# A planner inside the kernel: VectorE and GpSimd excluded from each other, new durations, and layer 0's leftover work carried into layer 1's plan

## The chip, the core and the metric

The kernel runs on one core of one Trainium2 chip. The metric is the device time of one launch in microseconds (us); the median of three runs is used. Short names: PE is TensorE (matmuls), DVE is VectorE, ACT is ScalarE, POOL is GpSimd, SP is SyncE, which only issues DMAs here.

## The reference

One inference step of a two-layer decoder trunk with model width 1024, in fp32, on 1056 tokens: a prompt of 1024, and 8 samples of 4 tokens that go on from given states. Each layer computes `x + mixer(rmsnorm(x) @ w_in) * silu(gate) @ w_out`; a last rmsnorm follows.

- Layer 0 is an RG-LRU. `w_in` maps 1024 to 2 x 1536 (the branch and its gate). The branch goes through a causal convolution of width 4 and through two gates (recurrence and input), each of 16 blocks of 96 x 96; then comes the scan `h[t] = a[t] h[t-1] + sqrt(1 - a[t]^2) * i[t] * x[t]` along the tokens, with `a = exp(-8 softplus(-lambda) r)`.
- Layer 1 is an HGRN2 with 8 heads. `w_in` maps 1024 to 4 x 1024 (q, f, i, gate). Per head a state of 128 x 128 is carried along the tokens with a decay per row, and `o = q S`. An rmsnorm per head, the silu gate and `w_out` follow.

Outputs are both `y` and the new states of both layers.

## The kernel before

**Data and products.** Everything is held transposed: 128 features on the partitions, tokens along the free axis, in three chunks of `CH` = 352 tokens. fp32 accuracy comes from three fp32r matmuls per product step (`mm3`, lines 243 to 245): each operand is split into a rounded part (`xh`, `whi`) and a rest (`xl`, `wlo`), and high x high, low x high and high x low are summed in PSUM. A product of 128 output features has 8 such steps (k = 0 to 7). Weights come by DMA (line 312), ACT casts them to `whi` (line 380), and DVE or POOL subtracts to give `wlo` (line 325, the helper `subtract`, which also makes every `xl`).

**Start of layer 0.** PE has 48 small filler matmuls (line 729), most of which run ahead of the first product. Two DMAs bring the gains and the packed parameters `P`. For chunk 0, ACT and DVE make `xh` and `xl` from the raw x (lines 861, 867), and the norm's factor is put in after the product; for chunks 1 and 2 the norm's factor is put in before. `squares` (lines 430, 432, 435) squares each x and adds up; a matmul sums over the partitions (line 279); DVE scales (line 447), POOL takes the power -1/2 (line 449), DVE builds a diagonal (lines 450, 453) and PE spreads it over the partitions (line 455). `scaled_parts` then does for each k: DVE scale (line 460), ACT cast (line 461), DVE or, for k = 3 and 7, POOL subtraction (line 325). The products are evacuated (line 482), convolved (ACT line 498, then three DVE steps on line 501) and split (lines 506, 507), or turned into gates (lines 529 to 534). `lru` (from line 539) holds the block gates, the tanh, exp and sqrt on ACT and the scan. `smalls`, `smalls1` and `masks` are 46 tiny DVE operations, with some on ACT and POOL, on `P` (tile "smalls"); they are recorded through the helper `seq` (line 734).

**Entry to layer 1.** Layer 0 ends with `out_last` and `first1` (line 708), which computes the first two projections of head 0 of layer 1; line 721 on POOL writes the gate rows `ST` (called `Gs` in layer 1). In layer 1, `own_gate` and `scale` (lines 1023 to 1045) multiply rows of a head by decays, level by level (line 1064 combines the gate rows). PE then runs four "bursts" of small matmuls per head (lines 1330 to 1345): burst 1 for levels 0 and 1, burst 2 for levels 2 and 4, burst 3 for levels 8 and 16, burst 4 for levels 32 and 64. The first three are made of `diag` (line 1052), burst 3 of `emit16` (line 1106) as well; DVE keeps their results (lines 1056, 1059) and scales the rows for the next burst. From head `HC` = 2 on, the projections use seven products in place of eight on halved token blocks (`seven`, line 1501 for the sums of their results); for these, `build` makes 56 sums of inputs on DVE (line 1368) and splits them (`parted_sum`, lines 1371 and 325).

**What sets the order.** No order is written out by hand. Every operation is recorded by `fl.add(engine, us, emit, reads, writes, prio, ...)` into a `Flow` (line 52), with an estimated duration `us` and keys that it reads and writes; dependencies come from the keys. There are two Flows, one for layer 0 with `first1`, and one for layer 1 with the tail. `Flow.run` (line 185) then orders all operations at build time:

- `plan` (line 102) is a greedy list scheduler: the engine that can start earliest takes, of its operations that are ready, the one with the smallest key. `lag` adds a hop between engines, and DMAs add a latency. `both` marks DVE operations that must not run beside POOL's: such an operation is planned longer if POOL is busy when it starts.
- `back` (line 140) plans backward and returns latest starts, which become the keys of the next plan; this is done 8 times and the best plan is kept.
- `search` (line 167) shifts the keys of a few operations planned in the first 60 us at random, 3000 times, and keeps what brings a chosen later PE operation forward. Only layer 0 uses it (`fl.run(SEARCH, 60.0)`); layer 1 calls `fl.run()`.

The order so found is what each engine's instruction stream has; nothing is reordered on the chip. Main products keep their order among each other (`main=True`); other PE work (block gates, bursts, norms) is placed between them.

Of the kernel before, what the change touches and what calls it, by code (L numbers as in the profile page):

```python
# [19 lines left out]
ALU = mybir.AluOpType  # L20
# [31 lines left out]
class Flow:  # L52
# [3 lines left out]
    HOP = 0.2  # L56
# [38 lines left out]
    def lag(self, i, j):  # L95

        a, b = self.ops[i], self.ops[j]
        if a[0] == b[0] and not a[5]:
            return 0.0
        return self.HOP + b[6] + (2.15 + a[5] / 250.0 if a[5] else 0.0)  # L100

    def plan(self, key, stop=None):
# [5 lines left out]
        free = dict.fromkeys(self.ENGINES, 0.0)  # L108
        dma = 0.0
# [4 lines left out]
        for _ in range(n):  # L114
# [6 lines left out]
            if both and free["POOL"] > t0:  # L121
                us = max(us, free["POOL"] - t0 + us - 0.13)
# [89 lines left out]
def tile_trunk(ctx: ExitStack, tc: tile.TileContext, xT, prm, hc, w0, wg, wo0, w1, wo1, s_in,  # L212
# [85 lines left out]
    with ExitStack() as l0:  # L298
# [92 lines left out]
        def product(w, xs, step=8, more=()):  # L391
# [3 lines left out]
            for s in range(0, n, step):  # L395
# [6 lines left out]
                fl.add("PE", 0.48 * len(ks), emit, (*(q for k in ks for q in (*xs[k][2], *w(k)[2])), *more), (pk,), 1, main=True)  # L402
# [34 lines left out]
        def norm(acc, own=None):  # L437
# [11 lines left out]
            fl.add("POOL", 1.2, lambda: G.tensor_tensor(r[:, :3], r[:, :3], mhalf[:, :3], op=ALU.pow), (rk,), (rk,), 0)  # L449
# [14 lines left out]
        def conv(g, head=False):  # L464

            items = []
            for j in range(3):
# [3 lines left out]
                def evac(c, ps, pk, by=None, j=j, m=m, mine=mine):  # L471
# [25 lines left out]
                    for src, dst, sh, u in parts:  # L497
                        act(u, lambda src=src, dst=dst, sh=sh: S.activation(dst, sh(src, 3), AF.Identity, bias=pc("cb", m),  # L498
                                                                         scale=pc("cw", 36 + m)), (xk, ("P",)), (tk,), 1, 0.1)
# [39 lines left out]
        def lru(g):  # L539
# [11 lines left out]
            for c in range(NCH):  # L551
# [5 lines left out]
                for i, hb in ((0, hbr), (1, hbi)):  # L557
                    for j in range(3):
# [7 lines left out]
                                                                           scale=0.5), (pk, ("sm",)), (("R", s, i, j),), 2, 0.05)  # L566
# [5 lines left out]
                                                            scale=0.5), (pk, ("sm",)), (("td", i),), 2, 0.05)  # L572
# [3 lines left out]
                for j in range(3):  # L576
                    m = 3 * g + j
                    act(CH, lambda j=j, m=m, ta=ta, ab=ab: S.activation(ab[:, j], ta[:, j], AF.Exp, bias=cn[:, m:m + 1], scale=cn[:, m:m + 1]),
                        (tak[j], ("sm",)), (("a", s, j),), 3, 0.15)
                    act(CH, lambda j=j, m=m, ta=ta: S.activation(ta[:, j], ta[:, j], AF.Tanh, bias=cp[:, m:m + 1], scale=cp[:, m:m + 1]),  # L580
                        (tak[j], ("sm",)), (tak[j],), 3, 0.15)
# [6 lines left out]
                act(3 * CH, lambda ta=ta: S.activation(ta, ta, AF.Sqrt, scale=0.25), tak, tak, 3, 2.6)  # L588
# [3 lines left out]
                for j in range(3):  # L592
# [12 lines left out]
                    fl.add("DVE", 0.9, lambda h=h, aj=aj, bj=bj, p=p: V.tensor_tensor_scan(h, aj, bj, p, op0=ALU.mult, op1=ALU.add),  # L605
# [1206 lines left out]
```

## Time and profile before

| what | value |
|---|---|
| three runs | 1072.68, 1069.47, 1072.2 us; median 1072.2 |
| profiled execution | 1069.42 us, of which the span of the instructions is 1067.3 |
| mean granted TensorE clock | 0.996 of full speed |
| instructions | 25614 |
| HBM | 71.05 MB read, 25.49 MB written |
| DMA | 103.06 MB, 97 GB/s on average |

How to read it: the span is the time from the first to the last recorded instruction, and the profiled execution's own time lies about 2 us above it. The page gives the busy time of each engine; a view by stretches gives the same for parts of the span, and a timeline gives the instructions of one engine in order, each run of like instructions with its start, its busy time, its line and shape and, in brackets, the idle time ahead of it with the instruction that ended it. A start that the text takes from a timeline is the first number of its row.

### The profile page before, as it was taken

The numbers are of one execution on the slowest core, as the hardware profiler recorded it, in microseconds if no ns is written. First come the engines' busy times: TensorE is split into PE (matmuls) and PEld (weight loads), VectorE is DVE, ScalarE is ACT, GpSimd is POOL, SyncE is SP. The second block draws the span as 40 slices with busy tenths as digits, with TensorE's granted clock in tenths as the row PEclk, the third lists the DMA queues.
The fourth block names the chain that finished last, engine by engine and source line by source line (L and its number), as shares of the span: only waits on it lengthen the run. The fifth ranks groups of instructions, "written<-read, shape, count | busy, mean of one in ns | idle before, by whom it ended". The sixth has DMA issues, their size and how long they took to land.

```text
span 1067.3 us, 25614 instructions
## 1 busy us (share of the span) xinstructions
PE 1054.5 (99%) x9964; PEld 1026.1 (96%) x9964; DVE 816.2 (76%) x1610; ACT 589.2 (55%) x1340; POOL 526.4 (49%) x601
## 2 busy tenths in 40 slices
PE   9999999999999999999989999999999999999997
PEld 9999999999999999999989999999999999999986
DVE  7999995788888689264798987877868686883436
ACT  6569656877675875243344464646464554652324
POOL 3426443444634365555657555555545455552544
PEclk9999999999999999999999999999999999999998
DMA  9201112123752585440211121212121212374204
GB/s 294 67 20 52 57 47 74 56 60 97 228 173 61 171 282 179 126 131 28 80 33 40 44 91 46 90 44 91 44 92 51 74 62 65 123 214 127 78 8 163
DMA packets 70120, 103.06 MB, mean 97 GB/s; under 512 B 9200, under 2 KB 50160, under 8 KB 70000
## 3 DMA queue, kind: packets, MB, share of 16 engines
q1 hardware_dynamic: 67696, 98.67, 29.6%
q10 hardware_dynamic: 2304, 2.77, 0.7%
q8 instruction: 78, 1.28, 0.5%
q14 instruction: 42, 0.34, 0.1%
HBM read 71.05 MB, written 25.49 MB: 90 GB/s over the span
## 4 chain that ended last, share of the span: by engine, by line
PE 90%; DVE 6%; issue 1%; DMA 1%; POOL 1%; ACT 0%; ACTq 0%; POOLq 0%; DVEq 0%
PE mm L243 25%; PE mm L244 24%; PE mm L245 24%; PE hg L1052 1%; PE hg L569 1%; PE hg L1271 1%; DVE R L1368 1%; PE hg L1217 1%; PE hg L1161 1%; PE hg L243 1%; PE hg L245 1%; PE hg L244 1%; PE hg L1273 1%; DMA wraw<-in_w_dram 1%; PE mm L1052 1%
## 5 line engine op out<-in xcount | busy, mean ns | idle before, releaser
L243 PE MATMUL mm<-xh,whi 128*128 128x352 f32 (+1 forms) x1143 | 359.5, 315 | 0.0
L244 PE MATMUL mm<-xl,whi 128*128 128x352 f32 (+1 forms) x1143 | 354.8, 310 | 0.0
L245 PE MATMUL mm<-xh,wlo 128*128 128x352 f32 (+1 forms) x1143 | 354.7, 310 | 0.0
L325 POOL TENSOR_TENSOR wlo<-wraw,whi 128x256 fp32r<-128x256 f32 (+3 forms) x184 | 199.2, 1100 | 189.7 <-ACT whi L380 104.5
L244 PEld LDWEIGHTS mm<-xl,whi 128*128 128x128 f32 x1143 | 215.8, 189 | 1.7
L243 PEld LDWEIGHTS mm<-xh,whi 128*128 128x128 f32 x1143 | 215.5, 189 | 1.8
L245 PEld LDWEIGHTS mm<-xh,wlo 128*128 128x128 f32 x1143 | 215.5, 189 | 0.0
L501 DVE SCALAR_TENSOR_TENSOR k<-xb,prm_sb,k 128x352 f32<-128x352 f32 (+2 forms) x144 | 89.2, 629 | 14.8 <-ACT k L498 10.8
L243 PE MATMUL mm<-t,whi 128*128 128x264 f32 (+1 forms) x306 | 89.4, 292 | 0.5 <-DVE k L1501 0.5
L244 PE MATMUL mm<-t,whi 128*128 128x264 f32 (+1 forms) x306 | 87.7, 287 | 0.0
L245 PE MATMUL mm<-t,wlo 128*128 128x264 f32 (+1 forms) x306 | 87.6, 286 | 0.0
L1501 DVE TENSOR_TENSOR k<-mm,k 128x264 f32<-128x264 f32 x144 | 60.4, 428 | 34.5 <-PE mm L245 32.7
L584 POOL TENSOR_TENSOR k<-X 128x352 f32<-128x352 f32 x36 | 44.4, 1243 | 45.1 <-DVE R L585 34.3
L325 POOL TENSOR_TENSOR wlo<-R,whi 128x256 fp32r<-128x256 f32 x64 | 51.8, 830 | 25.4 <-ACT whi L1428 25.4
L380 ACT CAST whi<-wraw 128x512 fp32r<-128x512 f32 (+2 forms) x83 | 45.9, 574 | 26.4 <-PE mm L244 18.7
L243 PEld LDWEIGHTS mm<-t,whi 128*128 128x128 f32 x306 | 57.6, 188 | 1.2 <-DVE k L1501 0.9
L245 PEld LDWEIGHTS mm<-t,wlo 128*128 128x128 f32 x306 | 57.6, 188 | 0.0
L244 PEld LDWEIGHTS mm<-t,whi 128*128 128x128 f32 x306 | 57.6, 188 | 0.0
L243 PE MATMUL mm<-yh,whi 128*128 128x352 f32 x153 | 49.9, 326 | 0.0
L1428 ACT CAST whi<-wraw 128x512 fp32r<-128x512 f32 x52 | 32.0, 616 | 31.7 <-PE mm L245 17.4
L244 PE MATMUL mm<-yl,whi 128*128 128x352 f32 x153 | 49.4, 323 | 0.0
L245 PE MATMUL mm<-yh,wlo 128*128 128x352 f32 x153 | 49.4, 323 | 0.0
(478 smaller groups left out, 2601.3 us busy)
## 6 DMA issues: line engine op xcount, KB each, us to landing
wraw<-in_w_dram SPq DMA_DIRECT2D x90, 256.0 KB, 2.7
wraw<-in_wo_dram SPq DMA_DIRECT2D x34, 192.0 KB, 2.5
si<-in_s_in_dram SPq DMA_DIRECT2D x8, 512.0 KB, 3.6
out_ss_out_dram<-si SPq DMA_DIRECT2D x8, 512.0 KB, 2.8
R<-in_w_dram SPq DMA_DIRECT2D x15, 256.0 KB, 2.5
sg<-x1b SPq DMA_DIRECT2D x21, 176.0 KB, 2.8
x<-sg SPq DMA_DIRECT2D x21, 176.0 KB, 1.8
R<-td SPq DMA_DIRECT2D x72, 44.0 KB, 1.9
```

The costliest lines, as they stand in the source:

```text
L243: T.matmul(out, wh, xh, start=first, stop=False)
L244: T.matmul(out, wh, xl, start=False, stop=False)
L245: T.matmul(out, wl, xh, start=False, stop=last)
L325: emit = lambda: e.tensor_tensor(b, x, a.bitcast(F32), op=ALU.subtract)
L380: act(m, lambda hi=hi, raw=raw, m=m: S.copy(hi[:, :m], raw[:, :m]), rk, (hk,), prio)
L501: dve(u, lambda src=src, dst=dst, sh=sh, k=k: V.scalar_tensor_tensor(dst, sh(src, k), pc("cw", 12 * k + m), dst, op0=ALU.mult, op1=ALU.add ...
L569: fl.add("PE", 0.62, lambda ps=ps, i=i, c=c: T.matmul(ps[:96, :CH], gs[:, i, :], ST[:96, chunk(c)], start=True, stop=True), (("gs",), *((" ...
L584: pool(CH, lambda x=x, a=a, b=b: G.tensor_tensor(x, a.bitcast(F32), b.bitcast(F32), op=ALU.add), (ak, bk), (xk,), 3)
L1052: T.matmul(ps[32 * j:32 * j + 32, n * w:n * w + w], B[:, o:o + 32], q(slice(o, o + 32)), start=True, stop=True, tile_position=(0, 32 * j))
L1161: T.transpose(ps[:, n * 128:(n + 1) * 128], row[:, a:a + 128], ident)
L1428: act(512, lambda: S.copy(hi, raw), (rk,), (hk,), 2)
L1501: dve(QT, lambda: V.tensor_tensor(o[0], z[0], u[0], op=ALU.add), (z[1], u[1]), (o[1],), 0)
```

## The change

Nothing that is computed changes; the figures by which the two Flows order the operations do.

1. **Exclusion.** A `both` operation used to be stretched by what was left of POOL's operation at its start. Now it works both ways: a `both` operation of DVE is planned longer by what is left of POOL's last operation (`taken`), and a POOL operation by what is left of the last `both` operation (`locked`). The allowance is 0.085 and 0.05 in place of 0.13.
2. **Durations.** The estimates of ACT, DVE and POOL as functions of the columns n, the hop between engines, and the costs of many single operations are set anew. `seq`, used by the small parameter operations, falls from 0.2 to 0.1 and its DVE operations lose the mark `both`. POOL's `tensor_scalar` in `first1` and in layer 1 falls to 0.3 of its length, its `memset` rises from 0.3 to 0.7.
3. **Leftover work.** Layer 1's Flow starts each engine not at zero but at the time by which its last planned operation of layer 0 ends after PE's (`busy`). An operation of POOL with no instruction and no duration writes the gate keys `GK`.
4. **Search.** Layer 1's Flow runs the random search over its first 60 us, as layer 0's did.

The list of operations that are recorded and their dependencies are otherwise the same. `SEARCH` stays at 3000.

```diff
-    HOP = 0.2
+    HOP = {"PE": 0.22, "DVE": 0.14, "ACT": 0.14, "POOL": 0.14, "SP": 0.2}
...
-    def __init__(self, until=None, side=1.2):
+    def __init__(self, until=None, side=1.2, busy=None):
...
+        self.busy = {e: (busy or {}).get(e, 0.0) for e in self.ENGINES}
...
-        return self.HOP + b[6] + (2.15 + a[5] / 250.0 if a[5] else 0.0)
+        return self.HOP[a[0]] + b[6] + (2.15 + a[5] / 250.0 if a[5] else 0.0)
...
-        free = dict.fromkeys(self.ENGINES, 0.0)
-        dma = 0.0
+        free = dict(self.busy)
+        dma = locked = taken = 0.0
...
-            if both and free["POOL"] > t0:
-                us = max(us, free["POOL"] - t0 + us - 0.13)
+            if both:
+                us += max(0.0, taken - t0 - 0.085)
+                locked = t0 + us
+            elif e == "POOL":
+                us += max(0.0, locked - t0 - 0.05)
+                taken = t0 + us
...
         def act(n, emit, r, w, prio=5, more=0.0):
-            fl.add("ACT", 0.25 + 0.0007 * n + more, emit, r, w, prio)
+            fl.add("ACT", 0.08 + 0.00086 * n + more, emit, r, w, prio)

         def dve(n, emit, r, w, prio=5, both=False):
-            fl.add("DVE", 0.13 + 0.0011 * n, emit, r, w, prio, both=both)
+            own = 0.13 if "scalar_tensor_tensor" in emit.__code__.co_names else 0.075
+            fl.add("DVE", own + 0.00104 * n, emit, r, w, prio, both=both)

         def pool(n, emit, r, w, prio=5):
-            fl.add("POOL", 0.1 + 0.00245 * n, emit, r, w, prio)
+            fl.add("POOL", 0.13 + 0.0022 * n, emit, r, w, prio)
...
-                fl.add("PE", 0.48 * len(ks), emit, (*(q for k in ks for q in (*xs[k][2], *w(k)[2])), *more), (pk,), 1, main=True)
+                fl.add("PE", 0.484 * len(ks), emit, (*(q for k in ks for q in (*xs[k][2], *w(k)[2])), *more), (pk,), 1, main=True)
...
-            fl.add("POOL", 1.2, lambda: G.tensor_tensor(r[:, :3], r[:, :3], mhalf[:, :3], op=ALU.pow), (rk,), (rk,), 0)
+            fl.add("POOL", 0.9, lambda: G.tensor_tensor(r[:, :3], r[:, :3], mhalf[:, :3], op=ALU.pow), (rk,), (rk,), 0)
...
-                    pool(CH, lambda o=o, a=a, b=b: G.tensor_scalar(o[:, q], t, a[:, :1], b[:, :1], op0=ALU.mult, op1=ALU.add),
+                    pool(0.3 * CH, lambda o=o, a=a, b=b: G.tensor_scalar(o[:, q], t, a[:, :1], b[:, :1], op0=ALU.mult, op1=ALU.add),
...
-                fl.add(eng, 0.2, emit, (("P",),), keys, prio, both=eng == "DVE")
+                fl.add(eng, 0.1, emit, (("P",),), keys, prio)
...
-        fl = Flow(side=0.4)
+        last = {e: max(t[3] for t in fl.log if t[1] == e) for e in Flow.ENGINES}
+        fl = Flow(side=0.4, busy={e: max(0.0, t - last["PE"]) for e, t in last.items()})
...
-            pool(0.3 * n, lambda o=o: G.memset(o, 0.0), (), keys, 3)
+            pool(0.7 * n, lambda o=o: G.memset(o, 0.0), (), keys, 3)
...
+        fl.add("POOL", 0.0, lambda: None, (), GK, 0)
...
-            fl.run()
+            fl.run(SEARCH, 60.0)
```

The hunks left out change single estimates in the same way: tanh, exp and one cast 0.05 to 0.1 higher, the square root 2.6 to 2.5, the scan 0.9 to 0.85, and some ten PE costs of layer 1 by up to 0.16.

More of the change, by code (lines that the diff above doesn't have):

```diff
@@ L604, in lru @@
                     p, ppk = prev[j]
[L605 removed]
+                    fl.add("DVE", 0.85, lambda h=h, aj=aj, bj=bj, p=p: V.tensor_tensor_scan(h, aj, bj, p, op0=ALU.mult, op1=ALU.add),
                            (("a", s, j), tik[j], *((ppk,) if ppk else ())), (hk,), 3, both=True)
@@ L1171, in samples @@
             ps = s[:, a:a + 128]
-            pe(0.22, lambda: T.matmul(ps[:96], o, ident, start=True, stop=True), ((ok,),), (sk,))
+            pe(0.17, lambda: T.matmul(ps[:96], o, ident, start=True, stop=True), ((ok,),), (sk,))
             yield
@@ L1298, in outs @@
                     (("ssq", i),), (("rst", i),), 2)
-                fl.add("POOL", 0.85, lambda r=r: G.tensor_tensor(rst[:, r], rst[:, r], mhalf[:, r], op=ALU.pow),
+                fl.add("POOL", 0.95, lambda r=r: G.tensor_tensor(rst[:, r], rst[:, r], mhalf[:, r], op=ALU.pow),
                        (("rst", i),), (("rst", i),), 2)
@@ L1467, in emit @@
                             mm3(ps[:, :QT], (hi[:, w], lo[:, w]), uh, ul, j == 0, j == 3)
-                    pe(1.45, emit, (*wk, *(k for o in ops for k in o[2])), (pk,))
+                    pe(1.465, emit, (*wk, *(k for o in ops for k in o[2])), (pk,))
                     z = ps[:, :QT], pk
```

40 lines of the change are left out of this document (20 added, 20 removed).

## The prediction

> **What bounds the kernel now.** The page comes first: it tells which engine sets the time.
>
> ```profile
> PE 1054.5 (99%) x9964; PEld 1026.1 (96%) x9964; DVE 816.2 (76%) x1610; ACT 589.2 (55%) x1340; POOL 526.4 (49%) x601
> ```
>
> TensorE (PE) is busy for all but 12.8 us of the span of 1067.3. Both the order before and the order after hold the same PE instructions, so a new order can only change those 12.8 us and the clock. The busy times by stretch show where they lie.
>
> ```profile
> 0.00:46.00 46.00, 44.25 (x286) 43.29 (x287) 39.49 (x89) 28.61 (x60) 18.88 (x26) 1.00 0.65 209
> 46.00:540.00 494.00, 494.00 (x3208) 486.76 (x3207) 383.00 (x687) 303.34 (x599) 236.17 (x258) 1.00 0.34 104
> 540.00:552.00 12.00, 8.59 (x166) 8.18 (x166) 11.93 (x20) 4.48 (x9) 5.21 (x6) 0.86 0.15 47
> 552.00:1040.00 488.00, 487.47 (x6158) 468.88 (x6156) 364.84 (x778) 240.48 (x641) 254.25 (x298) 1.00 0.24 76
> 1040.00:1067.30 27.30, 20.16 (x155) 18.95 (x154) 16.98 (x39) 12.26 (x32) 11.88 (x16) 0.90 0.45 159
> ```
>
> The columns after the stretch and its length are PE, weight loads, DVE, ACT and POOL busy, then the granted clock. PE idles 1.75 us at the start, nothing from 46 to 540, 3.41 us where layer 1 begins, 0.53 us in the rest of layer 1 and 7.14 us in the tail. The waits of PE name what releases it at the start (those of the entry stand further down, in the timeline):
>
> ```profile
> PE mm L243 <- DVE sg L529: 0.4, 1, 0.4
> PE mm L244 <- DVE xl L325: 0.3, 1, 0.3
> ```
>
> Every one of them is DVE. DVE works 39.49 of the first 46 us. So two stages can move: the start, which DVE bounds with hardly any slack, and the entry to layer 1, where DVE is late for one burst.
>
> **The change, part by part.** The constants, the per-engine hop and the exclusion add no instruction: every engine holds the same set (two of ACT's table loads stand before another line). The empty POOL entry and the leftover times emit nothing. All cost is the new order, which I read from the order of the instructions in both built programs (line numbers of before).
>
> *Start: what moves.* Before the first real product PE now runs 32 fillers (L729) instead of 46; the other 16 come later, so PE's work is unchanged. What decides is DVE. PE's first product for the second token chunk needs eight scaled inputs; the last of them (k = 7) is an L460 on R, then ACT's cast, then POOL's subtraction. Before:
>
> ```profile
> 41.24 0.57 DVE L460 SCALAR_TENSOR_TENSOR R<-R,g,hg 128x352 f32<-128x352 f32 x1
> 41.73 0.95 DVE L325 TENSOR_TENSOR xl<-sg,xh 128x352 fp32r<-128x352 f32 x2
> 42.60 0.51 DVE L482 TENSOR_TENSOR xb<-mm,R 128x352 f32<-128x352 f32 x1
> 43.03 1.70 DVE L325 TENSOR_TENSOR xl<-sg,xh 128x352 fp32r<-128x352 f32 x3
> ...
> 45.10 1.19 DVE L501 SCALAR_TENSOR_TENSOR k<-xb,prm_sb,k 128x352 f32<-128x352 f32 x2
> 46.20 1.08 DVE L460 SCALAR_TENSOR_TENSOR sg<-sg,g,R 128x352 f32<-128x352 f32 x2
> ```
>
> ```profile
> 42.41 1.08 POOL L325 TENSOR_TENSOR xl<-R,xh 128x352 fp32r<-128x352 f32 x1 [0.61 <-ACT xh L461]
> ```
>
> ```profile
> 46.10 0.33 PE L243 MATMUL mm<-xh,whi 128*128 128x352 f32 x1
> ```
>
> That L460 gives way to the next instruction at 41.73, POOL ends 1.76 us later at 43.49, and the product ends where the next begins, 46.10.
>
> In the new order more DVE work stands ahead of the same L460. From the starts above, one L325 or L482 takes 0.43 us, one L501 0.55, one L460 0.50. The small parameter operations:
>
> ```profile
> 0.00:46.00 46.00, 2.60 (x14) 0.59 (x3) 0.00 (x0) 1.00 0.65 209
> 46.00:540.00 494.00, 5.76 (x32) 95.32 (x168) 6.42 (x6) 1.00 0.34 104
> ```
>
> These are the stretches for the tile "smalls", DVE in the first column: 32 of its 46 operations stood behind 46 us and took 5.76 us, 0.18 each. Now all 46 stand ahead. Counted against before, ahead of that L460 stand in addition: 6 L325 of 352 columns (2.6), 7 L501 (3.9), 2 L482 and, at the same cost, 2 L507 (1.7), 1 L460 and 1 L531 (1.0), the third chunk's norm, L450 with its shorter L447 and L453
>
> ```profile
> 27.71 0.42 DVE L450 TENSOR_TENSOR k<-ident,nr 128x256 f32<-128x256 f32 x1
> ```
>
> (0.7, an estimate), and the 32 small ones (5.3; 5.76 if none overlaps another). Sum 15.2 us. What can be won back is DVE's idle time and the time in which it stood still while busy:
>
> ```profile
> 3.70 0.17 DVE L774 TENSOR_TENSOR smalls<-prm_sb 128x8 f32<-128x8 f32 x1 [2.68 <-DMA prm_sb<-in_prm_dram]
> ...
> 6.79 1.08 DVE L867 SCALAR_TENSOR_TENSOR xl<-sg,g,xh 128x352 fp32r<-128x352 f32 x2 [1.63 <-ACT xh L861]
> ...
> 18.51 2.64 DVE L435 TENSOR_TENSOR xb<-xb,xo 128x352 f32<-128x352 f32 x2
> ```
>
> ```profile
> 19.18 1.59 POOL L325 TENSOR_TENSOR yl<-ST,yh 128x512 fp32r<-128x512 f32 x1
> ```
>
> From 3.70 to 46 DVE is idle for about 3.0 us (42.3 less 39.49 and a little that lies before 3.70). Of these I give back 2.5: the small operations fill the 1.63 and parts of the rest. Two L435 took 2.64 us instead of about 0.9 beside a POOL operation. Over the stage such stretching is about 6.9 us: 38.0 from 3.70 to 41.73, less 2.5 idle, less the plain durations (52 large operations at about 0.5, 14 small ones in 2.60). I take it as unchanged, since POOL has the same operations here and the 21 L435 are not among those that the plan holds apart from POOL; the other end is that all of it goes. The loads on SP and ACT are reordered too (x first, then weights); I take 0 for it, as DVE's queue is the longer.
>
> So the L460 ends at 41.73 + 15.2 - 2.5 = 54.4 (47.5 with all stretching gone, 56.9 with nothing won back), the product 2.3 us later (1.76 and three matmuls), at 56.7. Without a stall it would end at 46.1 + 1.6, for one L455 and two gate products now stand ahead of it on PE (0.6 + 2 x 0.5): 47.7. **Start: +9.0 us** (+2.1 to +11.5). PE cannot win this back: from 46 to 540 it has no idle time.
>
> [...]
>
> *Entry to layer 1: what moves.* Before, DVE waits and is late afterwards:
>
> ```profile
> 514.31 1.27 DVE L1064 TENSOR_TENSOR R<-R,ST 128x1056 f32<-128x1056 f32 x1 [7.58 <-POOL ST L721]
> ...
> 533.86 0.42 DVE L1368 TENSOR_TENSOR tmp<-xh,tmp 128x264 f32<-128x264 f32 x1
> ...
> 543.91 1.22 DVE L1034 TENSOR_TENSOR R<-R,sg 128x512 f32<-128x512 f32 x1
> ...
> 546.86 0.91 DVE L1056 COPY_PREDICATED attnd<-mask,hg 128x256 f32<-128x256 uint8 x2
> ```
>
> ```profile
> 538.08 0.75 PE L1052 MATMUL hg<-R,sg 128*32 128x32 f32 x64
> ...
> 545.79 0.76 PE L1052 MATMUL hg<-R,sg 128*32 128x32 f32 x64 [2.88 <-DVE sg L1034]
> 547.09 0.73 PE L1106 MATMUL hg<-R,a 128*16 128x16 f32 x64 [0.53 <-DVE a L1034]
> ...
> 548.50 0.49 PE L245 MATMUL mm<-xh,wlo 128*128 128x352 f32 x1
> 548.79 0.49 PE L243 MATMUL mm<-xh,whi 128*128 128x352 f32 x1
> ```
>
> DVE stands idle for 7.58 us behind POOL's L721, and from 533.86 to 543.91 it does 14 of the L1368 sums, due only for head 2, ahead of the scale for burst 3. Now 14 sums stand ahead of L1064, in that idle time (14 x 0.46 = 6.4 us), and two between burst 2 and the scale instead of 14. The scale may start when burst 2 has read its rows, at 538.8; its four L1034 took 543.91 to 546.86, 2.95 us, so they end at 541.8, and PE reaches burst 3 at 542.9. The stalls of 2.88 and 0.53 go, and with them the slow clock behind them: six matmuls at 0.29 instead of 0.16 us (estimate 1.0 in all). What is late next is burst 2: nine sums and four larger L1034 (0.6 to 1.2 each) follow burst 1, close to its 537.4; I take off 0.2. **Entry: -4.2 us** (-4.5 to 0).
>
> *The rest.* From 46 to 540 and in layer 1 the PE order hardly differs, and DVE is busy 78% and 75%; I take 0. It can't gain more than the 0.5 us idle; a new stall as long as the one above costs 3. In the tail the last chain's order is the same: 0.
>
> **Sum:** +9.0 - 4.2 = +4.8 us. The profiled execution took 1069.42 us (span 1067.3 and 2.1 around it), 2.8 below the median 1072.2 of the three runs (1069.47 to 1072.68). It becomes 1074.2; on the median, **1077.0**.
>
> **Rivals.** (A) *Not slower:* the start gives little away. If the collisions with POOL vanish from DVE's stage, the L460 ends at 47.5, PE loses 2.1, and the entry's 4.2 weighs more: -2.1, 1070.1. It decides at an L460 end of 49.6, where the loss is 4.2. For it speaks that the plan now holds marked operations apart; against it that L435 is unmarked. (B) *The entry's stall stays,* or moves to burst 2, so that part of the change does nothing: +9.0, 1081.2. Against it: the two sums left there against 14. (C) *Waits become slow clock, or new stalls:* by the same durations the start's waits come in pieces of up to 2.6 us, at k = 0, 1, 6 and 7; behind 2.88 us the trace showed 1.0 us lost. Two such, or one new stall later: +3, 1080. [...]
>
> **How the numbers follow.** Forecast 0.45, A 0.25, B 0.12, C 0.13, an outcome below A 0.05. About 0.3% (3.2 us) is what a measurement of this kernel tells from no change. Slower by more: B, C and most of the forecast, 0.62. Within: most of A, the forecast's lower edge, 0.26. Faster: 0.12. The range from 1069.5 (A near its best) to 1082 (B) leaves out 2 in 10.
>
> **What would show it.** In the changed profile: fillers in front of PE's first product end near 10.5 us; the L460 on R for chunk 1 starts near 54 and PE waits there for DVE or POOL, idle in the first 60 us near 10 us instead of 1.75. At the entry L1368 fills DVE's wait for L721, and no PE wait of 2.9 us on L1034 is left. I am wrong if PE's idle time before 60 us stays under 5 us, or if long waits appear between 60 and 500.

## The result: slower by 12.5 us, and the profile after

| kernel | median | runs | ratio to before, 95% interval |
|---|---|---|---|
| before | 1072.38 us | 1069.47 to 1072.68 (4) | |
| changed | 1084.88 us | 1083.88 to 1086.45 (4) | 1.0128 [1.0111, 1.0145] |

The direction was forecast, the size was not: +12.5 us on the medians against +4.8, and outside the range. The two profiled executions lie 16.3 us apart (1085.73 and 1069.42); that of before is 3.0 us under its median, the other 0.85 over its own, and 12.5 + 3.0 + 0.85 = 16.3. The stages below come from the two traces, so they add up to the larger figure.

In the changed kernel the lines named here stand 5 to 8 higher (the three matmuls of a step are L248 to L250): L435 is L441, L460 is L466, L325 is L331, L1034 is L1042, L1438 is L1446, L1501 is L1509. The engines' row of its page:

```profile
PE 1061.4 (98%) x9964; PEld 1028.2 (95%) x9964; DVE 804.4 (74%) x1610; ACT 592.3 (55%) x1340; POOL 513.6 (47%) x601
```

DVE and POOL are busy for less time than before (816.2 and 526.4), PE does the same 9964 matmuls, and the span is 16.6 us longer (1084.0 and 1067.3, rounded). So it is again an affair of PE's waits and clock. The busy times by stretch (PE, weight loads, DVE, ACT, POOL, then the granted clock):

```profile
0.00:46.00 46.00, 40.47 (x238) 38.29 (x239) 40.52 (x115) 26.36 (x55) 16.82 (x24) 0.93 0.65 209
46.00:60.00 14.00, 12.45 (x72) 11.19 (x71) 13.93 (x31) 7.66 (x17) 3.25 (x9) 1.00 0.03 7
60.00:100.00 40.00, 37.18 (x215) 35.92 (x214) 37.69 (x83) 28.36 (x57) 13.81 (x16) 0.96 0.10 28
...
548.00:562.00 14.00, 13.63 (x326) 13.00 (x325) 13.28 (x26) 6.46 (x16) 8.69 (x7) 1.00 0.13 41
562.00:1056.00 494.00, 488.43 (x6157) 468.41 (x6155) 361.26 (x782) 243.17 (x642) 248.55 (x298) 1.00 0.23 75
```

In the first 100 us PE is idle for 5.53 + 1.55 + 2.82 = 9.9 us (1.75 before) and runs at 0.93 and 0.96 of its clock in two of the stretches (1.00 before). At the entry to layer 1, 548 to 562, idle time and slow clock are gone: 0.37 us are left of 3.41. In the rest of layer 1 PE is idle for 5.57 us, where it was 0.53.

Both kernels run the main products in the same order, so the start of the same matmul in both timelines gives the **lag** of the changed kernel at that point. Three such matmuls, the last but one group of layer 0, the first products behind the entry, and one near the end; first before, then changed:

```profile
537.03 0.32 PE L244 MATMUL mm<-xl,whi 128*128 128x352 f32 x1
...
552.37 0.32 PE L244 MATMUL mm<-xl,whi 128*128 128x352 f32 x1
...
979.59 0.32 PE L244 MATMUL mm<-xl,whi 128*128 128x352 f32 x1
```

```profile
551.44 0.33 PE L249 MATMUL mm<-xl,whi 128*128 128x352 f32 x1
...
562.60 0.32 PE L249 MATMUL mm<-xl,whi 128*128 128x352 f32 x1
...
995.91 0.32 PE L249 MATMUL mm<-xl,whi 128*128 128x352 f32 x1
```

The lag is 14.4 us ahead of the entry, 10.2 behind it and 16.3 near the end. **Layer 0 costs 14.4, the entry gives back 4.2, the heads of layer 1 cost 6.1.** The tail adds 0.3 to reach the 16.6 of the spans.

What PE waits for, longest sum first (sum, times, longest):

```profile
PE mm L248 <- DVE k L1509: 3.4, 6, 0.6
PE hg L249 <- DVE X L513: 2.8, 1, 2.8
PE hg L284 <- DVE R L441: 2.5, 2, 1.9
PE mm L249 <- DVE xl L331: 1.2, 2, 0.6
```

**Layer 0.** Two things on DVE stand in the way. First the norm of chunk 0, in DVE's timeline:

```profile
27.62 1.45 DVE L747 TENSOR_SCALAR smalls<-smalls 128x12 f32<-128x12 f32 x2
28.98 0.49 DVE L747 COPY smalls<-smalls 32x4 f32<-32x4 f32 x3
29.49 0.15 DVE L453 TENSOR_SCALAR nr<-hg 96x1 f32<-96x1 f32 x1
29.67 1.59 DVE L441 TENSOR_TENSOR R<-R,xo 128x352 f32<-128x352 f32 x3
...
31.79 1.63 DVE L441 TENSOR_TENSOR R<-R,xo 128x352 f32<-128x352 f32 x1
33.34 0.41 DVE L456 TENSOR_TENSOR k<-ident,nr 128x256 f32<-128x256 f32 x1
...
55.23 0.58 DVE L466 SCALAR_TENSOR_TENSOR R<-R,g,hg 128x352 f32<-128x352 f32 x1
```

```profile
56.43 0.93 POOL L331 TENSOR_TENSOR xl<-R,xh 128x352 fp32r<-128x352 f32 x1 [2.86 <-ACT xh L467]
```

Small parameter operations stand ahead of the last norm step L453, and sums of L441, one of them stretched from about 0.5 to 1.63 us beside POOL, ahead of the diagonal L456. The diagonal comes at 33.34; it came at 27.71 before. The L460 whose place the prediction worked out, the one whose result goes through ACT to POOL's subtraction at 56.43, starts at 55.23, 14.0 us later than before. Then, later in the same timeline, masks and a wait of PE:

```profile
69.84 0.94 DVE L805 TENSOR_SCALAR k<-k 128x32 int32<-128x32 int32 x1
...
79.27 2.97 DVE L507 SCALAR_TENSOR_TENSOR k<-xb,prm_sb,k 128x352 f32<-128x352 f32 x3
...
87.14 0.52 DVE L513 TENSOR_TENSOR X<-k,X 128x352 fp32r<-128x352 f32 x1
```

```profile
87.71 0.43 PE L249 MATMUL hg<-X,gh 128*128 128x352 f32 x1 [2.82 <-DVE X L513]
...
90.97 0.49 PE L248 MATMUL hg<-X,gh 128*128 128x352 f32 x1
```

From 69.84 to 79.27 DVE does the masks of layer 1 (L805, 33 operations, most of them some 0.2 us from start to start) and five other operations (2.6 us); the convolution behind them brings X at 87.7, and PE stands for 2.82 us. That the masks cause this wait is read from the order; no run moved them alone. Behind it a matmul of the gates takes 0.49 us in place of 0.32: the granted clock is 0.5 from 88.9 us on, for 3.41 us.

**Layer 1.** The same wait comes back in five heads. DVE, then POOL, then PE around one of them:

```profile
657.23 0.43 DVE L1509 TENSOR_TENSOR k<-mm,k 128x264 f32<-128x264 f32 x1
657.58 2.03 DVE L1446 TENSOR_TENSOR wraw<-wraw 128x512 f32<-128x512 f32 x1
659.54 0.42 DVE L1509 TENSOR_TENSOR sg<-mm,k 128x264 f32<-128x264 f32 x1
659.88 0.42 DVE L1509 TENSOR_TENSOR k<-mm,k 128x264 f32<-128x264 f32 x1
```

```profile
655.59 2.08 POOL L1203 TENSOR_TENSOR vb<-vst,bm 96x256 fp32r<-96x256 f32 x2 [4.07 <-DVE vst L1185]
657.63 3.26 POOL L331 TENSOR_TENSOR wlo<-wraw,whi 128x256 fp32r<-128x256 f32 x4
```

```profile
660.35 0.39 PE L248 MATMUL mm<-t,whi 128*128 128x264 f32 x1 [0.62 <-DVE k L1509]
```

L1446 sums parts of weights, both inputs in SBUF; with no operation of POOL beside it, it takes 0.68 us. Here it starts 0.09 us ahead of the end of a POOL operation and takes 2.03: two more operations of POOL (0.73 and 0.74 us) begin and end before it does. The two sums L1509 that free PE's bank are late by that, and PE waits 0.62 us. It happens at the same place of five heads. The sixth wait of the list (0.32 us, in the last head) is not new; the same one is in the kernel before:

```profile
PE mm L243 <- DVE k L1501: 0.5, 1, 0.5
```

The lag grows by 0.56 us at the first of the five and by 0.88 at each of the others, 4.1 in sum. Most of the rest of the 6.1 lies at four other waits of 0.3 to 0.9 us (584.3, 588.1, 836.8 and 959.0), the longest in front of a burst (L1060).

### The profile page after: what moved, and what is told of

It is laid out like the page before. It is cut to its first block, busy times and chain, and to the rows that moved or that the text cites. A ratio compares the mean times of both kernels' runs of the same rounds, so it can differ in the third digit from the quotient of the medians.

```text
span 1084.0 us, 25607 instructions
## 1 busy us (share of the span) xinstructions
PE 1061.4 (98%) x9964; PEld 1028.2 (95%) x9964; DVE 804.4 (74%) x1610; ACT 592.3 (55%) x1340; POOL 513.6 (47%) x601
## 4 chain that ended last, share of the span: by engine, by line
PE 82%; DVE 10%; issue 3%; DMA 2%; ACT 2%; POOL 1%; ACTq 0%; POOLq 0%; SPq 0%; DVEq 0%
PE mm L248 23%; PE mm L250 22%; PE mm L249 22%; PE hg L1060 1%; PE hg L575 1%; DVE sg L466 1%; DVE xl L331 1%; PE hg L1279 1%; PE hg L1225 1%; PE hg L249 1%; PE hg L1281 1%; PE hg L250 1%; PE hg L248 1%; DMA wraw<-in_w_dram 1%; PE hg L1169 1%
## 5 line engine op out<-in xcount | busy, mean ns | idle before, releaser
L248 PE MATMUL mm<-xh,whi 128*128 128x352 f32 (+1 forms) x1143 | 358.6, 314 | 0.0
L250 PE MATMUL mm<-xh,wlo 128*128 128x352 f32 (+1 forms) x1143 | 354.8, 310 | 0.3 <-POOL wlo L331 0.3
L331 POOL TENSOR_TENSOR wlo<-wraw,whi 128x256 fp32r<-128x256 f32 (+3 forms) x184 | 188.8, 1042 | 204.1 <-ACT whi L386 118.0
L248 PEld LDWEIGHTS mm<-xh,whi 128*128 128x128 f32 x1143 | 215.3, 188 | 1.5
L250 PEld LDWEIGHTS mm<-xh,wlo 128*128 128x128 f32 x1143 | 215.6, 189 | 0.6 <-POOL wlo L331 0.6
L248 PE MATMUL mm<-t,whi 128*128 128x264 f32 (+1 forms) x306 | 89.9, 294 | 3.4 <-DVE k L1509 3.4
L1509 DVE TENSOR_TENSOR k<-mm,k 128x264 f32<-128x264 f32 x144 | 60.2, 426 | 38.5 <-PE mm L250 37.9
L250 PE MATMUL mm<-t,wlo 128*128 128x264 f32 (+1 forms) x306 | 87.5, 286 | 0.0
L331 POOL TENSOR_TENSOR wlo<-R,whi 128x256 fp32r<-128x256 f32 x64 | 51.6, 826 | 32.4 <-ACT whi L1436 31.4
L248 PEld LDWEIGHTS mm<-t,whi 128*128 128x128 f32 x306 | 57.6, 188 | 4.9 <-DVE k L1509 4.7
L250 PEld LDWEIGHTS mm<-t,wlo 128*128 128x128 f32 x306 | 57.7, 189 | 0.0
L248 PE MATMUL mm<-yh,whi 128*128 128x352 f32 x153 | 51.4, 336 | 0.0
L250 PE MATMUL mm<-yh,wlo 128*128 128x352 f32 x153 | 49.4, 323 | 0.0
```

The source lines that it names most:

```text
L248: T.matmul(out, wh, xh, start=first, stop=False)
L250: T.matmul(out, wl, xh, start=False, stop=last)
L331: emit = lambda: e.tensor_tensor(b, x, a.bitcast(F32), op=ALU.subtract)
L1509: dve(QT, lambda: V.tensor_tensor(o[0], z[0], u[0], op=ALU.add), (z[1], u[1]), (o[1],), 0)
```

## The experiments

Every kernel is compared with the kernel before on the same chip; its lag is taken at the three matmuls above. The edits are to the planner's figures, so each kernel computes the same. Sixteen ran.

All lags count from the one trace of before, and its execution (1069.42 us) was some 3 us shorter than the median of before in these comparisons. A kernel that is as fast as before on the medians therefore shows a lag of some 3 us near the end. Where this comes from can be seen in part: l1_only and left_only, with layer 0 in the order of before, are 0.9 and 1.0 us late ahead of the entry, and four kernels with PE's order of before in layer 1 (before_draw2, before_draw3, l0_only and seq_only) change their lag by -0.5 to +2.7 us from there to the near end. So a lag says where time is lost, and the medians say how much. One source is in the traces. In the first of the five heads the order of before has a sum L1438 that stands through two POOL operations in the trace of before, without a wait of PE, and through four in that of before_draw2, where PE then waits 2.0 us (first before, then before_draw2; l0_only has 3.28 us too):

```profile
646.07 1.91 DVE L1438 TENSOR_TENSOR R<-wraw,R 128x512 f32<-128x512 f32 x1
```

```profile
650.71 3.28 DVE L1438 TENSOR_TENSOR R<-wraw,R 128x512 f32<-128x512 f32 x1
```

**One layer at a time.** l0_only plans layer 0 as the changed kernel does and layer 1 as before; l1_only the other way round (the functions `act`, `dve`, `pool`, the hop and the exclusion switch by the Flow that they record for). The few costs written in helpers of both layers, such as that of a product step, go with layer 0, so the order within layer 1 is not quite the one meant: PE's is the same, or all but the same, while about 100 (l0_only) and 160 (l1_only) of DVE's 870 operations stand at another place.

```diff
-        fl = Flow("PE")
+        fl = Flow("PE", new=False)     # l1_only; l0_only: Flow(side=0.4, new=False)
```

> Layer 0 is planned as in the changed kernel, layer 1 as before (old estimates, old exclusion, no leftover times, no search). If the losses add up stage by stage (theory: the start costs 14.4 us by the lag of equal matmuls in the two traces, the entry gives 4.2 back, the heads of layer 1 cost 6.0), the lag at the end of layer 0 is again about 14.4 us, the entry gives nothing back, the heads cost nothing, and the median lies 12 to 15 us above before, near 1086. Rival: the loss in the heads is caused by layer 0's leftover state and comes along: 1090 or more.

> Layer 0 is planned as before, layer 1 as in the changed kernel (new estimates, two-way exclusion, leftover times, search). Theory of stages: no lag before the entry, the wait of 2.9 us on the scale for burst 3 is gone, the short waits on L1501's sums are there: -4.2 + 6.0 = +1.8 us, near 1074. Rival: the waits of 0.6 us per head hang on something in layer 0 of the changed kernel and are absent: -4.2, near 1068.

Measured: l0_only 1082.76 us (1.0092 [1.0075, 1.0109]), lags 12.5, 12.5 and 13.8; l1_only 1073.45 us (1.0006 [0.9996, 1.0015]), lags 0.9, -3.0 and 4.4. The two layers are separate: the start's loss is layer 0's alone (12.5 and not 14.4 us in this execution of the same order: the wait for X took 0.8 us and not 2.8), and both the entry's gain and the heads' loss come with the plan of layer 1 alone, whose waits are in l1_only too:

```profile
PE mm L252 <- DVE k L1513: 3.2, 6, 0.6
```

On the medians l0_only loses 10.0 us, less than the 12 to 15 expected, and l1_only 0.7; together 10.6 of the 12.5. The lag of 1.3 us that l0_only gains behind the entry is one wait of 2.0 us at 663.05, at the first of the five places.

**One edit undone in the changed kernel.**

```diff
 seq_back:
-                fl.add(eng, 0.1, emit, (("P",),), keys, prio)
+                fl.add(eng, 0.2, emit, (("P",),), keys, prio, both=eng == "DVE")
 excl_back:
-            if both:
-                us += max(0.0, taken - t0 - 0.085)
-                locked = t0 + us
-            elif e == "POOL":
-                us += max(0.0, locked - t0 - 0.05)
-                taken = t0 + us
+            if both and free["POOL"] > t0:
+                us = max(us, free["POOL"] - t0 + us - 0.13)
```

> The changed kernel with one edit undone: the small parameter operations are planned at 0.2 us and with the mark again. Theory A (the price of 0.1 us hides about 0.1 us of DVE work for each of some 89 operations, smalls and masks, which the plan then puts ahead of urgent work): the lag at the end of layer 0 falls from 14.4 to under 5 us, the median to 1073 to 1076. Theory B (the two-way exclusion) and theory C (the shorter estimates of ordinary operations and hops, which leave no slack): the lag stays over 10 us, 1081 to 1085.

> The changed kernel with the exclusion of before (one direction, allowance 0.13 us) in both layers. Theory B: the lag at the end of layer 0 falls under 5 us and the waits on L1501's sums go, median near 1066 to 1072. Theories A and C: the lag of layer 0 stays over 10 us, 1080 to 1086.

Measured: seq_back 1077.38 us (1.0047 [1.0032, 1.0062]), lags 8.4, 4.3 and 10.3. It gains 7.5 us; the lag of layer 0 is 8.4, between the two forecasts. excl_back 1091.14 us (1.0171 [1.0155, 1.0186]): 6.3 us slower than the changed kernel and slower than any of the theories allowed, with a lag of layer 0 of 15.0; its entry has the long wait again (2.9 us on L1034's counterpart). Theory B falls in this form: in this company the two-way rule is a gain.

**One part alone, put into the kernel before.** seq_only has the 0.1 us without the mark, excl_only the two-way exclusion, dur_only the new durations and hops, left_only the leftover times, the empty operation and the search in layer 1; the edits are the hunks shown in the section on the change.

```diff
 left_only:
-        fl = Flow(side=0.4)
+        last = {e: max(t[3] for t in fl.log if t[1] == e) for e in Flow.ENGINES}
+        fl = Flow(side=0.4, busy={e: max(0.0, t - last["PE"]) for e, t in last.items()})
...
+        fl.add("POOL", 0.0, lambda: None, (), GK, 0)
...
-            fl.run()
+            fl.run(SEARCH, 60.0)
```

> The kernel before with one part of the change: the small parameter operations are planned at 0.1 us without the mark. Theory A1 (this price alone puts too much on DVE's early stage): lag at the end of layer 0 of 5 to 9 us, median 1077 to 1081. Rival A2 (the price hurts only together with the shorter estimates, which leave no slack to hide it in): lag under 2 us, 1071 to 1074. Layer 1 keeps its order of before, so nothing may change behind the entry.

> The kernel before with one part of the change: the two-way exclusion, in both layers. Undoing it in the changed kernel cost 6.3 us, so theory B' (the two-way rule by itself is a gain) says 1066 to 1072, with at most a small lag in layer 0. Rival B'' (the two-way rule brings the six waits of 0.6 us on L1501's sums, which were gone where it was undone): +4 to +6 us in layer 1, 1076 to 1079.

> The kernel before with one part of the change: the new estimates of durations and hops, with the small parameter operations at 0.2 us and marked, the one-way exclusion, no leftover times and no search in layer 1. Theory C (the shorter estimates leave no slack): lag at the end of layer 0 of 6 to 9 us, as with the small operations' price undone (7.0), and further waits in layer 1: 1080 to 1088. Rival: the estimates by themselves move little, 1070 to 1075, and the losses need the other parts.

> The kernel before with one part of the change: the leftover times, the empty operation on the gate keys and the search in layer 1. Layer 0 is as before. Four of the L1368 sums stand ahead of L1064 in place of none (14 in the changed kernel), and 12 ahead of the first keep in place of 16. Theory D (the leftover times are what ends the wait of 2.9 us on the scale for burst 3): -3 to -4.5 us, 1068 to 1070. Rival: the gain of 4.2 needs the new estimates as well, and the wait stays or moves: 1071 to 1074.

| kernel | median | ratio, 95% interval | lag before the entry, behind it, near the end |
|---|---|---|---|
| seq_only | 1077.24 us | 1.0039 [1.0024, 1.0054] | 6.5, 6.7, 6.0 |
| excl_only | 1079.25 us | 1.0062 [1.0047, 1.0078] | 6.6, 2.2, 9.0 |
| dur_only | 1085.16 us | 1.0117 [1.0102, 1.0133] | 9.4, 12.5, 16.5 |
| left_only | 1067.34 us | 0.9951 [0.9934, 0.9968] | 1.0, -2.6, -2.1 |

Against the 1072.82 of these runs the parts give +4.4, +6.4, +12.3 and -5.5 us, 17.7 in sum for a whole of 12.5. They don't add, which was to be expected of a planner. But their order is plain: the new durations cost most, and the leftover work alone is a gain. seq_only and dur_only came out near theories A1 and C, left_only gained more than theory D said. Theory B' falls: alone, the two-way rule is a loss. excl_only did not bring the waits of the five heads either, as B'' said; its loss in layer 1 is another, a set of three waits at one place with slow matmuls behind the last (0.59 us, where those behind the first two took 0.40 and 0.39), of which the longest is

```profile
632.80 0.59 PE L247 MATMUL mm<-xh,whi 128*128 128x264 f32 x1 [1.56 <-ACT xh L1375]
```

Of the waits on L1501's sums dur_only and excl_back, which have the new durations and the one-way exclusion, show three (1.6 us in sum), none of them at one of the five places. All five stand in every kernel that has the new durations and the two-way exclusion in layer 1 (each has the leftover part as well), add_long further down excepted; of the others, three have a wait at the first place alone (l0_only, before_draw2 and before_draw3). A stretched sum is not enough for a wait: dur_only has one of 2.14 us in each of the five heads, and PE does not wait there. dur_only has, at the entry, a wait twice as long as that of before:

```profile
558.62 1.08 PE L1054 MATMUL hg<-R,sg 128*32 128x32 f32 x64 [6.30 <-DVE sg L1036]
```

In left_only the timeline of DVE still shows the wait for the gate rows, 7.41 us in place of 7.58, and yet PE's wait of 2.9 us is down to 0.4 and 0.5:

```profile
PE hg L1109 <- DVE R L1037: 0.5, 1, 0.5
PE hg L1055 <- DVE R L1037: 0.4, 1, 0.4
```

So filling DVE's idle time isn't needed for the gain. What changed is that five of L1368's sums, and not 14, stand between the scale for burst 2 and the scale for burst 3, which starts at 541.19 and not at 543.91. left_only holds three edits, and which of them moves the sums wasn't told apart.

**Is it only another draw of the search?** All three parts that reach layer 0 made it later. That could mean that the order of before is a lucky draw.

```diff
-        rng = Random(1)
+        rng = Random(2)      # before_draw3: 3
```

> The kernel before, nothing changed but the seed of the random search (2 in place of 1), which reorders the start of layer 0 alone; all estimates, the price of 0.2 us and the one-way exclusion stay, layer 1 keeps its order. All three parts of the change that reach layer 0, taken alone, put the end of its first stage 5 to 9 us later. Theory E (the order of before is one draw of the search that comes out well on the chip, and any change of a figure draws another): start lag of 3 to 9 us here too, median 1076 to 1082. Theory of causes (price, exclusion and estimates are each worse in themselves): start lag within 1.5 us, 1071 to 1074.

> The same with seed 3. Theory E: again 3 to 9 us late, 1076 to 1082. Theory of causes: within 1.5 us, 1071 to 1074.

> The changed kernel with seed 2. Theory E: its start lag is another draw, anywhere from 3 to 15 us, and need not be near 14.4; the entry and the six waits of 0.6 us per head in layer 1 stay, as the search doesn't reach them: 1074 to 1086. Theory of causes: the lag at the end of layer 0 stays at 12 to 16 us, 1083 to 1087.

Measured: before_draw2 1074.16 us (1.0016 [1.0007, 1.0025]), lag of layer 0 3.0; before_draw3 1070.47 us (0.9978 [0.9969, 0.9987]), lag 0.3; after_draw2 1087.92 us (1.0139 [1.0124, 1.0154]), lag 17.7, more than either theory named, and again the waits of the five heads. Theory E falls as an account of the whole: other draws move the median by 1.5 and 2.2 us with the figures of before, and by 3.0 with those of the change, whose start is late with both seeds tried. before_draw2's 3.0 lies at the edge of what E named, so a draw is worth something: of a single part's +4.4 or +6.4, some 2 us may still be the draw.

**Which figure makes the start late?**

```diff
 mark_only, and with seq_back's edit seq_mark:
-... a[:, :CH], sq, op=ALU.add), (sk, ak), (ak,), 2)
+... a[:, :CH], sq, op=ALU.add), (sk, ak), (ak,), 2, *(() if e is G else (True,)))
```

> The changed kernel with the small operations planned at 0.2 us and marked again, and with L435's sums on DVE marked as well, which are 3.9 us longer than their shortest in the first 60 us, each time beside an operation of POOL that had started before. If the plan's missing mark causes the rest of the start's loss (7.0 us with the price alone undone): lag at the end of layer 0 under 4 us, 1072 to 1075. Under theory E it is one more draw: lag of 3 to 10 us, 1074 to 1081.

> The changed kernel with L435's sums on DVE marked and the small operations still planned at 0.1 us without the mark. With both edits the lag at the end of layer 0 was 2.6 us, with the price alone 8.4, with none 14.4. If the missing mark has a share of its own (some 6 us): lag of 7 to 10 us, 1077 to 1081. Rival (the mark counts only once the price is right): lag of 12 to 15, 1083 to 1087. Layer 1 has the order of the changed kernel.

Measured: mark_only 1077.35 us (1.0051 [1.0036, 1.0066]), lag of layer 0 6.0 us; seq_mark 1074.14 us (1.0017 [1.0007, 1.0026]), lags 2.6, -1.4 and 4.4. Of the 14.4 us the price alone takes 6.0 away, the mark alone 8.4, both 11.8; a draw of the search may be some 3 us of each. The mark does not make the sums faster: in seq_mark, too, three of L441's sums take 2.90 us together, and they still stand right ahead of the diagonal:

```profile
26.48 2.90 DVE L441 TENSOR_TENSOR R<-R,xo 128x352 f32<-128x352 f32 x3
29.30 0.41 DVE L456 TENSOR_TENSOR k<-ident,nr 128x256 f32<-128x256 f32 x1
```

The diagonal starts at 29.30 (33.34 in the changed kernel, 27.71 before). What differs is how much stands ahead of it: 48 operations of DVE, 12 of them small ones, where the changed kernel has 86 with 46 small ones. The mark alone does that too (49 with 13, mark_only's diagonal starts at 26.80); the price alone does not (73 with 35, seq_back's starts at 34.87). At the product that starts at 46.10 before, mark_only is 1.7 us late, seq_mark 1.2, seq_back 7.9 and the changed kernel 11.8; from there to the end of layer 0 mark_only loses 4.3 more, seq_mark 1.5, seq_back 0.4 and the changed kernel 2.7. So the mark clears the start, and the price counts for more in the stretch behind it. Of the small operations (tile "smalls", DVE first) 12 stand in the first 46 us of seq_mark and not 46:

```profile
0.00:46.00 46.00, 1.70 (x12) 0.60 (x3) 0.00 (x0) 1.00 0.61 198
```

**Which figure makes the waits in the five heads?** add_long is seq_mark with the sums of weights planned as long as they are beside POOL.

```diff
-                dve(512, lambda: V.tensor_tensor(o, x, y, op=op), (xk, yk), (ok,), 2, True)
+                fl.add("DVE", 1.4, lambda: V.tensor_tensor(o, x, y, op=op), (xk, yk), (ok,), 2)
```

> The changed kernel with the small operations at 0.2 us and marked, L435's sums marked, and with one more estimate changed, in layer 1: the sums of weights (L1446 of the changed kernel) are planned at 1.4 us, the mean of those 16 that stood beside POOL operations on both sides, without the mark. Theory F (the six waits of 0.6 us per head come from this sum, planned at 0.6 to 0.8 us as if it went ahead of POOL's next operation, while it took 2.03 us on the chip each time): the waits on L1509 go, the lag grows by less than 2 us from the entry to the tail in place of 6, 1068 to 1071. Rival: other waits come in their place, 1073 to 1076.

Measured: 1069.94 us (0.9982 [0.9973, 0.9992]), lags 2.9, -1.7 and 0.2. Behind the entry it loses 1.9 us, where seq_mark lost 5.8. The waits of the five heads are gone:

```profile
PE mm L248 <- DVE k L1509: 1.1, 2, 0.8
```

Of these two the shorter (0.31 us) is that of the last head, and the longer (0.83 us, at 647.19) is new, at another place and behind another sum that took 2.39 us beside POOL. So the waits of the five heads came from how these sums were planned. The edit changes their length and their mark together; which of the two is needed wasn't told apart.

**Do the gains add up?** left_mark is left_only with the mark on L435, left_draw3 is left_only with seed 3.

```diff
 left_mark: left_only's and mark_only's edits;  left_draw3: left_only's edits and Random(3)
```

> The kernel before with the leftover times, the gate key operation and the search in layer 1 (1067.3 us) and L435's sums on DVE marked. If the missing mark is a fault of the kernel before too: the start is 0 to 2 us earlier, 1065 to 1068. Rival (with the one-way exclusion and the long estimates the mark brings nothing): the start is 1 to 4 us later, 1068 to 1071.

> The kernel before with the leftover times, the gate key operation and the search in layer 1, and seed 3 of the search in both layers. Seed 3 alone gave 1070.5 beside 1072.6, the leftover part alone 1067.3 beside 1072.8. If the two add up: 1064.5 to 1066. Rival: seed 3 draws a worse order for the entry, 1067 to 1070.

Measured: left_mark 1067.28 us (0.9957 [0.9942, 0.9972]), left_draw3 1067.08 us (0.9954 [0.9938, 0.9971]). Neither can be told from left_only's 1067.34. The mark brings nothing to the figures of before (lag of layer 0 1.6 us); seed 3 kept its start (0.4) but has a wait of 1.3 us at the entry. The leftover part by itself is the version to keep, some 5 us faster than before and 17.5 faster than the changed kernel.

## Why the prediction was right or wrong

**The start, +9.0 forecast.** The sum nearly held at the place where it was made. The L460 gave way to the next instruction at 55.72 (forecast 54.4). Ahead of it DVE was busy for 14.9 us more than before (forecast 15.2), and its idle time fell by 1.25 us (forecast 2.5). That the 15.2 came so close is partly luck: in the first 46 us the small operations cost 7.3 us more (9.88 in place of 2.60) and not 5.3, and the eight L867 together took some 1.5 us less than before, which nobody had counted on. The product that was to end at 56.7 ended at 57.85, where the next begins:

```profile
57.42 0.43 PE L249 MATMUL mm<-xl,X 128*128 128x352 f32 x1 [0.58 <-POOL xl L331]
57.69 0.33 PE L250 MATMUL mm<-xh,X 128*128 128x352 f32 x1
57.85 0.32 PE L248 MATMUL mm<-xh,whi 128*128 128x352 f32 x1
```

That is 11.75 later than before, or 10.2 without the 1.6 us of PE work that moved ahead of it. PE's idle time in the first 60 us was 7.1 us and not near 10; two stretches of slow clock of 3.41 us, which the sum had not, took 3.4 more. What was missed in layer 0 lies behind that point: the wait of 2.82 us for X at 84.9, behind the masks, and the slow clock that follows it (0.96 of 40 us, 1.6 us). 10.2 + 2.8 + 1.6 = 14.6, for 14.4 measured. A long wait between 60 and 500 was the prediction's own sign of being wrong. It counted the operations of the tile "smalls" (the 46 of `smalls` and `smalls1`) and not the masks, 33 more, which use the same helper and were made as cheap; and it took 0 from 46 us on.

**Why it is late at all.** The prediction counted the moved operations without asking which figure moved them. The runs answer: the price of 0.1 us for operations that take about 0.2 from start to start, and sums that the plan takes for 0.44 us and that take up to 1.65 beside POOL. L435 has no mark in the plan, and in the trace its sum takes 1.63 us beside POOL and about 0.5 without; mark_only shows what the missing mark cost: 7.5 us of the changed kernel, less or more by a draw. The prediction took the blank on L435 only as a reason for the stretching to stay as it was; it was one of the causes of the loss too.

**The entry, -4.2 forecast, -4.2 measured.** Burst 3's wait and the slow clock behind it are gone, as forecast. That the figure fits to the tenth is luck: l1_only, with the same change, gained 3.9. And left_only has most of it (3.6) with 7.41 us of DVE's idle time unfilled, so of the two reasons given the second (few sums between burst 2 and the scale) is enough, and the first is not needed.

**The rest, 0 forecast, +6.1 measured in layer 1.** This is the step that failed: "From 46 to 540 and in layer 1 the PE order hardly differs, and DVE is busy 78% and 75%; I take 0." PE's order does not tell when DVE frees PE's banks. The order of DVE within a head had changed, and a change there repeats with every head: one wait of 0.62 us in five heads, 4.1 us of lag in sum (from 11.57 ahead of the second to 12.45 behind it, for one), and four other waits for most of the rest. add_long shows the cause of the five: a sum of weights, planned as if it were short and 2.03 us long on the chip. The single new stall allowed for (3 us) was rival C's; there was one in layer 0 and nine small ones in layer 1.

**The rivals.** A needed POOL's collisions to vanish from the first stage; they didn't (L441 1.63 us), since the plan's exclusion changes what is planned and no instruction. B was wrong, the entry's stall went. C named the mechanism that decided, slow clock and new stalls, and priced it at 3 us in place of 2.8 + 1.6 + 6.1 = 10.5, the slow clock of the first 46 us not counted.

**What stays open.** In layer 0, some 2.6 us of lag in seq_mark, about the size of another draw; some 1 us of it is the fast execution from which lags count. Which edit of left_only ends the wait at the entry: the leftover times, the operation on the gate keys or the search. Why the new durations alone cost so much (dur_only, 12.3 us) is not settled line by line: argued, not shown, is that estimates without slack place urgent work just in time, and a collision that the plan doesn't see then reaches PE.

## What to carry to other kernels

A planner's figures are a whole: a better fit of one kind of operation makes the others' errors decide, as a price of 0.1 for 0.2 us and one missing mark did here (7.5 us each, taken back one at a time, of which a draw may be some 3). Where the order within a repeated stage changes on any engine, look for one new wait and multiply it by the repetitions before taking that stage at 0. Put parts of a change into the old kernel one by one: here three of four lost and the fourth alone was worth 5 us.

## What the runs showed of the hardware

**DVE's sums beside POOL.** In the traces of before and of the changed kernel, a sum on DVE with both inputs in SBUF (L435 and L1438; L441 and L1446) took longer when a square, a product or a subtraction of POOL was at work as it began (L1446: 0.79 to 2.03 us in 18 sums), and not when one began later. In the trace of before, the sums L435 took 0.52 us in the mean of 3 when POOL's operation began while they ran (a large one in one of the 3 only; five sums L1446 of the changed kernel took 0.68 us in that case, as they do alone), and 1.09 to 1.52 in the four that began while POOL was at a square (L430) or a subtraction (L325); L1501, which reads one input from PSUM, took 0.43 in both cases. Beside POOL's power on 128x3 elements they took no longer, though it is as long. Of the four sums in the second row, which took 1.84 us together, two began while it ran:

```profile
26.12 1.08 POOL L449 TENSOR_TENSOR nr<-nr,mhalf 128x3 f32<-128x3 f32 x1 [2.14 <-DVE nr L447]
25.96 1.84 DVE L435 TENSOR_TENSOR R<-R,xo 128x352 f32<-128x352 f32 x4
```

In these two traces six such sums began while a power of POOL was at work, as far as POOL's recorded spans go, and each took 0.52 to 0.53 us. L1446 also stood while POOL went on to its next operations. Starting 0.09 us ahead of the end of one POOL operation, it stood through the next two (0.73 and 0.74 us), at the same place of five heads; at 656.10, 0.56 us ahead of such an end, L1446 took 1.10 us and ended ahead of the end of POOL's next. DVE's own instruction ahead of the longer one ended within 0.01 us of POOL's; when POOL's second of the two began, L1446 had stood for 0.75 us. In before_draw2 the sum of 3.28 us shown above stood through four operations of POOL.

**The clock behind short waits.** In the first 46 us of the changed kernel no wait of PE is over 1.9 us, and the clock is 0.93: two stretches of 3.4 us at half speed. seq_back has four waits of 1.3 to 2.0 us and one of 0.8 in the same stretch, and no slow one:

```profile
0.00:46.00 46.00, 37.67 (x245) 35.79 (x246) 37.28 (x100) 26.68 (x54) 16.62 (x23) 1.00 0.66 209
```

So the sum of the waits doesn't decide. In the trace's record of the granted clock the slow stretches begin at 30.92, 41.16 and 88.94 us, 3 and 14 times 3.413 us apart; in the trace of before they begin at 546.56 and 1061.97, 151 times 3.413 us apart. In the 3.41 us ahead of the stretch at 41.16 PE was idle for 1.04 us; in seq_back it was idle for 1.89 us from 36.3 to 39.7, and the clock of its first 60 us is 1.00. So what brings on a slow stretch wasn't settled.
